# A two-block transformer kernel: operands of 16 and 64 rows become zero-padded operands of 128 rows

## The chip, the cores and the metric

The kernel runs on one core of a Trainium2 chip. The metric is device time in microseconds (us) of one execution, lower is better. Engines are named as in the profile: PE is the matrix engine (PEld its weight loads), DVE, ACT and POOL work on vectors, SP issues the DMAs.

## The reference

Two blocks run one after the other over 512 tokens with 16 meta tokens ahead of them (L = 528), width 1024, all in float32.

```python
def first_block(...):                       # two layers
    for i in range(2):
        xn = rms_norm(h, attn_norm[i])
        gq, gk, gv, gr, glr, fq, fk, fv, ff = split(xn @ w_in[i])
        log_a = log_sigmoid(glr @ w_alpha_up[i] + b_alpha[i]) / 16   # contracts over 16
        o_gla = gla_chunk_causal(gq, gk, gv, log_a)                  # 4 heads, chunks of 64 tokens
        log_f = log_sigmoid(ff + b_forget[i])
        o_fox = forgetting_attention(fq, fk, fv, log_f)              # 8 heads of 64, causal softmax
        h = h + concat(norm(o_gla) * silu(gr), norm(o_fox)) @ w_out[i]
        h = h + conv_ffn(rms_norm(h, ffn_norm[i]), ...)

def second_block(...):                      # one layer
    q, k, v, qi, ki, wi, cu, cb, cc, ga, gb = split(rmsnorm(h) @ w_in)
    score = einsum(relu(qi . ki), wi)       # 8 index heads of 64 features
    sel = top_k(score, 128)                 # keys that each query may see
    y_attn = softmax(q . k over sel) . v    # 8 heads of 128
    h = h + mixed(y_attn, short_conv branch) @ w_out
    h = h + gated_ffn(h)
```

## The kernel before

**Large products.** Each projection is a job: one 128-column tile of a weight matrix against all tokens, in `steps` (L291 to L322). Float32 operands are cut into a high and a low part of type fp32r, and each job adds hi*hi, hi*lo and lo*hi in one PSUM tile `mm`, at L309. A job of two 264-column halves and eight 128-row steps issues 48 matmuls.

**Side work.** Everything else (attention, gates, norms) is a queue of small functions. After every step of a job `pump` takes functions from that queue (a credit of `rate` for each step), so small products stand between the large ones on the same in-order PE. The tile framework's scheduler may shift an instruction a little; `pin` holds one in place. Operands lie in a pool of 64 slots of [128, 528] (`G`), small PSUM tiles in two pools of two (`PS`, `PT`).

**Small products with fewer than 128 rows.** A matmul contracts over the rows (partitions) of its two operands.

- Forgetting attention (FoX), four pairs of heads in each of two layers. A head has 64 features. `stacked_scores` (L494) does two matmuls: L497 has 128 rows (high and low queries stacked, keys' high parts in both halves), L498 has 64 rows (queries' high parts against the keys' low parts, which share one tile `kl` for both heads). L558 then adds the causal mask as a bf16 product of 128 rows. There is one unit of that kind for each head and query block: 2 heads x 5 blocks x 4 pairs x 2 layers = 80 units.
- FoX values (L608): two products over the 16 meta keys (`vms`, 16 rows) come first, then two of 128 rows for each key block, all in one PSUM tile. 32 such groups.
- FoX meta queries: a 16x16 transpose (L568) and a 16-row product (L574, a float32 product, which the engine runs as two instructions), 16 units.
- Index scores (L1070) use `stacked_scores` too, 40 times; nothing but large products follows.
- Attention of block 2: `attend_p` (L451) transposes each key block of the probabilities (L459) and the meta keys apart (L467, 16 columns); the product with the meta values (`dvm`, 16 rows) comes last at L1120, as two instructions, 32 groups.
- Gates (L391, 16 rows), the first block of each norm spread (L210, 16 rows) and the meta block in `fox_tail` (L669, 16 rows).

GLA's own products (L695, L709, L753, L760) have 16 or 64 rows too, and so have the transposes at L1561, L783 and L1191.

POOL zeroes the meta block of the FoX output tile (L524) and one block of the values' operand (L582) and does a few additions and powers. It works in order.

Of the kernel before, what the change touches and what calls it, by code (L numbers as in the profile page):

```python
# [8 lines left out]
F32 = mybir.dt.float32  # L9
# [6 lines left out]
META = 16  # L16
# [20 lines left out]
class Net:  # L37
# [43 lines left out]
    # ---------------------------------------------------------------- constants  # L81
    def constants(self):
# [26 lines left out]
        self.wa = c.tile([16, 2, 256], F32, name="wa")  # L109
# [48 lines left out]
    # ---------------------------------------------------------------- small helpers  # L158
# [34 lines left out]
    def token_sums(self, acc):  # L193
        """Per-token sums over the features: [128, 5], one column a token block."""
# [6 lines left out]
    def spread(self, r):  # L201
        """[128, L] tile with r's per-token values in every partition."""
# [3 lines left out]
        for j, (b, sz) in enumerate(BLK):  # L206
            dg = self.M()
            nc.vector.tensor_scalar(dg[:sz, :sz], self.ident[:sz, :sz], r[:sz, j:j + 1], None, op0=ALU.mult)
            t, o = (tiles[0], b) if b < HALF else (tiles[1], b - HALF)
            nc.tensor.matmul(t[:, o:o + sz], lhsT=self.ones[:sz, :], rhs=dg[:sz, :sz], start=True, stop=True)  # L210
# [10 lines left out]
    def norm_at(self, first, sums, spread):  # L221
        """A phase's norm factors, made while its first two jobs run: sums late in the first, spread in the second."""
# [4 lines left out]
    # ---------------------------------------------------------------- weight jobs  # L227
# [17 lines left out]
    def split(self, jb, pin=False):  # L245
        """High and low parts of a job's weights; a packed job has both in one tile, 64 columns each."""
# [20 lines left out]
    def push_unit(self, stages):  # L267
        """Stages of one unit of side work; each stage goes one unit later than the stage before it."""
# [22 lines left out]
    def steps(self, jb):  # L291
        """One job's matrix products, a step for each 128 rows of the weights, then its evacuation."""
# [31 lines left out]
    def run(self, look=2, ahead=4):  # L324
        """The jobs in order; the first two go together, as their operand comes in bit by bit."""
# [25 lines left out]
    def v(t, toks):  # L351
        """View of a [128, L] tile that matches psv of the same tokens."""
# [8 lines left out]
    def scaled(self, ps, toks, rs, out=None, extra=None):  # L361
        """ps * rs (* extra) over the tokens, into a slot."""
# [76 lines left out]
    def to_tokens(self, src, dst, dmeta, mcol, eng):  # L439
        """[128 features, L] -> four 128-token blocks side by side, and the meta rows."""  # L440
# [10 lines left out]
    def attend_p(self, P, j, qs, vt, vm, mcol, vw, vc):  # L451
        """Transposes of the probabilities' key blocks; gives (lhsT-ready) blocks."""
        nc = self.nc
        blocks = []
        if j:
            pt = self.PT("attend_pT_")
            for k in range(1, j + 1):
                b, _ = BLK[k]
                nc.tensor.transpose(pt[:, 128 * (k - 1):128 * (k - 1) + qs], P[:qs, b:b + 128],  # L459
                                    self.ident[:qs, :qs])  # L460
            PTs = self.G()
            self.copy("a" if j % 2 else "v", PTs[:, :128 * j], pt[:, :128 * j])
            for k in range(1, j + 1):
                blocks.append((PTs[:, 128 * (k - 1):128 * (k - 1) + qs],
                               vt[:, 128 * (k - 1) + vc:128 * (k - 1) + vc + vw]))
        pm = self.PT("attend_pT_")
        nc.tensor.transpose(pm[:META, :qs], P[:qs, :META], self.ident[:qs, :qs])  # L467
        PM = self.M()
        self.copy("v", PM[:META, :qs], pm[:META, :qs])
        blocks.append((PM[:META, :qs], vm[:META, mcol:mcol + vw]))  # L470
        return blocks

    def fox_k(self, st, t):
        """Per head: the keys' high parts in both row halves; the low parts of both heads in one tile."""
        nc = self.nc
        st["kl"] = kl = self.G(F32R)
        st["kh"] = []
        for b in range(2):
            R, O = slice(64 * b, 64 * b + 64), slice(64 - 64 * b, 128 - 64 * b)
            kh = self.G(F32R)  # L480
# [3 lines left out]
            st["kh"].append(kh)  # L484

    def stack_q(self, t, b, t0=0):
        """One head's queries: high parts in its own rows, low parts in the other rows."""
# [6 lines left out]
    def stacked_scores(self, ps, q, kh, kl, b, q0, a, n, stop):  # L494
        """Query rows q0.. against keys a..a+n, as high and low parts."""
        R = slice(64 * b, 64 * b + 64)
        self.nc.tensor.matmul(ps[:, :n], lhsT=q[:, q0:q0 + 128], rhs=kh[:, a:a + n], start=True, stop=False)  # L497
        self.nc.tensor.matmul(ps[:, :n], lhsT=q[R, q0:q0 + 128], rhs=kl[R, a:a + n], start=False, stop=stop)  # L498
# [1135 lines left out]
```

## Time and profile before

| | |
|---|---|
| timed runs, median of 3 | 2444.22 us (2442.56 to 2447.89) |
| profiled execution, span from first to last instruction | 2443.0 us |
| PE busy | 2411.0 us, 99% of the span |
| DVE, ACT, POOL busy | 1372.8, 942.0, 228.7 us |
| granted PE clock, mean | 0.994 of full speed |

The profile gives the span of its execution and no other time for it; the span lies 1.2 us under the median of the timed runs. A busy PE is not a PE at its peak: matmuls overlap, and the duration of one (some 280 ns for 264 columns) is not what it adds to the time. What it adds is read from the starts: from the start of one matmul to the start of the next.

### The profile page before, as it was taken

The page shows a single profiled execution, that of the slowest core. Times are in us where ns is not written, and L with a number is a line of the kernel's source. Part 1 is how long each engine was busy: PE and PEld are TensorE (multiplying, and loading weights), DVE is VectorE, ACT ScalarE, POOL GpSimd, SP SyncE. Part 2 cuts the span into 40 slices and gives each one's busy share as a digit, 9 for nine tenths or more (in the row PEclk, how much of TensorE's full clock was granted, in tenths as well). Part 3 has the DMA queues.
Part 4 walks back from the last instruction along what each step waited for, and adds up shares of the span by engine and source line. Part 5 has one row for each costly group of instructions (what it writes and reads, how often), then busy time and mean ns, then how long its engine had stood idle before and what let it go on. Part 6 is the DMA issues. An engine that isn't in the chain of part 4 may idle for free.

```text
span 2443.0 us, 37854 instructions
## 1 busy us (share of the span) xinstructions
PE 2411.0 (99%) x15831; PEld 2154.9 (88%) x15831; DVE 1372.8 (56%) x2492; ACT 942.0 (39%) x1609; POOL 228.7 (9%) x216
## 2 busy tenths in 40 slices
PE   7999999999999999999999999999999999999998
PEld 6888999999998888999898988888898888888888
DVE  6556656555555666566464664688344544433335
ACT  6553434333345544434232443332233523222225
POOL 1010110000021101200000031110000002101012
PEclk9999999999998999999999999999999999999999
DMA  4211122232331111222323222232221132232233
GB/s 123 57 53 36 53 87 87 91 100 78 100 85 52 49 39 53 70 87 87 104 83 100 81 90 70 70 104 87 87 69 53 56 100 87 88 102 87 95 99 126
DMA packets 217074, 196.79 MB, mean 81 GB/s; under 512 B 8987, under 2 KB 214791, under 8 KB 216903
## 3 DMA queue, kind: packets, MB, share of 16 engines
q1 hardware_dynamic: 216903, 194.37, 25.7%
q8 instruction: 125, 2.05, 0.4%
q14 instruction: 46, 0.38, 0.1%
HBM read 192.26 MB, written 2.10 MB: 80 GB/s over the span
## 4 chain that ended last, share of the span: by engine, by line
PE 67%; ACT 1%; issue 1%; DVE 1%; POOL 0%; DMA 0%; POOLq 0%; ACTq 0%; SPq 0%; DVEq 0%
PE mm L309 59%; PE valuesT L1120 1%; PE foxV L608 1%; PE scoresS L1103 1%; PE foxS L498 1%; PE idx L498 1%; PE gla_statesS L709 0%; PE foxT L588 0%; PE attend_pT L459 0%; PE spreadS L210 0%; ACT wh L260 0%; PE foxS L497 0%; PE idx L497 0%; PE to_tokensT L445 0%; PE foxS L558 0%
## 5 line engine op out<-in xcount | busy, mean ns | idle before, releaser
L309 PE MATMUL mm<-g,wh 128*128 128x264 f32 (+3 forms) x9168 | 1890.1, 316 | 6.8 <-DVE g L365 4.5
L309 PEld LDWEIGHTS mm<-g,wh 128*128 128x128 f32 x9168 | 1389.5, 190 | 124.2 <-issue 9.8
L309 PE MATMUL mm<-g,wl 128*128 128x264 f32 (+3 forms) x4552 | 1161.8, 313 | 0.0
L309 PEld LDWEIGHTS mm<-g,wl 128*128 128x128 f32 x4552 | 751.3, 189 | 51.6 <-issue 0.3
L260 ACT ACTIVATE wh<-raw 128x1024 fp32r<-128x1024 f32 (+1 forms) x369 | 384.6, 1043 | 978.6 <-PE mm L309 831.2
L261 DVE TENSOR_TENSOR wl<-raw,wh 128x1024 fp32r<-128x1024 f32 (+1 forms) x369 | 444.8, 1206 | 83.1 <-ACT wh L260 58.1
L365 DVE TENSOR_TENSOR g<-mm,g 128x528 f32<-128x528 f32 (+2 forms) x228 | 158.6, 696 | 327.5 <-PE mm L309 324.2
L191 POOL TENSOR_TENSOR g<-g,g 128x528 f32<-128x528 f32 (+3 forms) x49 | 71.5, 1470 | 911.8 <-ACT g L190 911.8
L166 DVE TENSOR_TENSOR g<-g,g 128x512 fp32r<-128x512 f32 (+3 forms) x131 | 91.5, 698 | 39.9 <-ACT g L972 29.0
L997 DVE TENSOR_TENSOR g<-mm,g 128x528 f32<-128x528 f32 (+1 forms) x48 | 33.6, 700 | 118.7 <-PE mm L309 118.6
L954 ACT ACTIVATE g<-g,cv 128x528 f32<-128x528 f32 (+1 forms) x88 | 72.1, 820 | 17.6 <-DVE g L365 17.6
L166 DVE TENSOR_TENSOR g<-foxT,g 16x128 fp32r<-16x128 f32 (+2 forms) x160 | 49.8, 335 | 42.9 <-ACT g L593 35.9
L957 DVE SCALAR_TENSOR_TENSOR g<-g,cv,g 128x526 f32<-128x526 f32 (+1 forms) x88 | 66.8, 760 | 3.1
L956 DVE SCALAR_TENSOR_TENSOR g<-g,cv,g 128x527 f32<-128x527 f32 (+1 forms) x88 | 66.3, 753 | 1.8 <-ACT g L954 1.8
L1383 POOL TENSOR_TENSOR g<-g,g 128x512 f32<-128x512 f32 x22 | 38.9, 1767 | 283.1 <-ACT g L1382 283.1
L968 ACT ACTIVATE g<-g 128x528 f32<-128x528 f32 (+1 forms) x44 | 28.1, 639 | 84.0 <-DVE g L957 84.0
L174 POOL TENSOR_TENSOR sm<-sm,mhalf 128x10 f32<-128x10 f32 (+4 forms) x29 | 36.8, 1279 | 192.5 <-DVE sm L173 192.1
L563 ACT ACTIVATE g<-g,sm 128x144 f32<-128x144 f32 (+2 forms) x80 | 41.4, 517 | 21.1 <-DVE sm L559 18.3
L593 ACT ACTIVATE g<-foxT 128x256 fp32r<-128x256 f32 (+1 forms) x96 | 32.8, 342 | 42.8 <-PE foxT L588 36.8
L970 DVE TENSOR_TENSOR g<-g,g 128x528 f32<-128x528 f32 (+1 forms) x44 | 30.8, 701 | 32.3 <-ACT g L968 32.3
L972 ACT ACTIVATE g<-g 128x528 fp32r<-128x528 f32 (+1 forms) x44 | 28.1, 639 | 33.1 <-DVE g L970 33.1
L1414 DVE TENSOR_TENSOR g<-mm,g 128x512 f32<-128x512 f32 x16 | 11.1, 692 | 50.2 <-PE mm L309 50.2
(264 smaller groups left out, 1699.0 us busy)
## 6 DMA issues: line engine op xcount, KB each, us to landing
raw<-in_w_up_dram SPq DMA_DIRECT2D x50, 1024.0 KB
raw<-in_w_in_dram SPq DMA_DIRECT2D x44, 1024.0 KB
raw<-in_w_down_dram SPq DMA_DIRECT2D x28, 896.0 KB
raw<-in_w_in_dram SPq DMA_DIRECT2D x28, 512.0 KB
raw<-in_w_out_dram SPq DMA_DIRECT2D x12, 1024.0 KB
raw<-in_w_down_dram SPq DMA_DIRECT2D x12, 1024.0 KB
raw<-in_w_gate_dram SPq DMA_DIRECT2D x10, 1024.0 KB
raw<-in_w_up_dram SPq DMA_DIRECT2D x10, 512.0 KB
```

Of the source, the lines that this page charges most:

```text
L166: (eng or self.nc.vector).tensor_tensor(out, x, hi.bitcast(F32), op=ALU.subtract)
L191: nc.gpsimd.tensor_tensor(acc[:, t0:t1], tmp[:, t0:t1], acc[:, t0:t1], op=ALU.add)
L260: keep(nc.scalar.activation(hi[:, :K], src, AF.Copy))
L261: keep(nc.vector.tensor_tensor(lo[:, :K], src, hi[:, :K].bitcast(F32), op=ALU.subtract))
L309: nc.tensor.matmul(ps[:, b, :n], lhsT=w[:, k, :], rhs=x[:, t:t + n], start=(ki == 0 and pi == 0), stop=(ki == len(order) - 1 and pi == len ...
L365: self.nc.vector.tensor_tensor(self.v(out, toks), self.psv(ps, toks), self.v(rs, toks), op=ALU.mult)
L498: self.nc.tensor.matmul(ps[:, :n], lhsT=q[R, q0:q0 + 128], rhs=kl[R, a:a + n], start=False, stop=stop)
L563: nc.scalar.activation(P[:qs, :N], P[:qs, :N], AF.Exp, scale=-1.0, bias=m, accum_out=col)
L954: nc.scalar.activation(A[:, lo:], U[:, lo:], AF.Identity, bias=self.vec("cb", 44 * i + t), scale=cw(2))
L956: nc.vector.scalar_tensor_tensor(A[:, s1:], U[:, s1 - 1:L - 1], cw(1), A[:, s1:], op0=ALU.mult, op1=ALU.add)
L957: nc.vector.scalar_tensor_tensor(A[:, s0:], U[:, s0 - 2:L - 2], cw(0), A[:, s0:], op0=ALU.mult, op1=ALU.add)
L1383: nc.gpsimd.tensor_tensor(z[:, META:], z[:, META:], self.rs[:, META:], op=ALU.mult)
```

## The change

Every operand named above gets 128 rows; the rows that were not there are zero, or meet a zero row of the other operand.

- `fox_k` makes one `kl` tile for each head, and POOL zeroes its other half (16 more memsets of 64x528, one more slot for each pair). L498 then has 128 rows.
- The meta values `fvm`, `fvms`, `dvm` are constant tiles of 128 rows, zeroed once by POOL at the start, of which rows 0 to 15 are written later. The probabilities that meet them are transposed 128 columns wide in place of 16.
- The meta-query unit works on 128 queries (its mask, softmax and transpose are 128 wide); the 16 that count are kept.
- `attend_p` transposes blocks of 128 columns only, up to four in one PSUM tile, the meta block first.
- Gates: `wa` has 128 rows, zero from row 16, and POOL zeroes rows 64 to 127 of `sm`. Spread and `fox_tail`: 128 rows.

GLA's own products and the transposes of the first tokens stay as they are.

```diff
+        self.wa = c.tile([128, 2, 256], F32, name="wa")
+        nc.gpsimd.memset(self.wa, 0.0)
+        for x in range(2):
+            self.fvm.append(c.tile([128, 128], F32, name=f"fvm{x}"))
...
+                nc.gpsimd.memset(t.bitcast(F32), 0.0)
...
-            nc.tensor.matmul(t[:, o:o + sz], lhsT=self.ones[:sz, :], rhs=dg[:sz, :sz], start=True, stop=True)
+            nc.tensor.matmul(t[:, o:o + sz], lhsT=self.ones, rhs=dg[:, :sz], start=True, stop=True)
...
-                nc.tensor.matmul(ps[:, :n], lhsT=self.wa[:, i, 128 * m:128 * m + 128], rhs=sm[:16, a:a + n],
+                nc.tensor.matmul(ps[:, :n], lhsT=self.wa[:, i, 128 * m:128 * m + 128], rhs=sm[:, a:a + n],
...
+        for x in range(0, j + 1, 4):
+            n = min(4, j + 1 - x)
             pt = self.PT("attend_pT_")
...
+            for k in range(n):
+                nc.tensor.transpose(pt[:, 128 * k:128 * k + 128], P[:, cols[x + k]:cols[x + k] + 128], self.ident)
...
         for b in range(2):
-            kh = self.G(F32R)
+            kh, kl = self.G(F32R), self.G(F32R)
+            nc.gpsimd.memset(kl[O, :].bitcast(F32), 0.0)
...
-        self.nc.tensor.matmul(ps[:, :n], lhsT=q[R, q0:q0 + 128], rhs=kl[R, a:a + n], start=False, stop=stop)
+        self.nc.tensor.matmul(ps[:, :n], lhsT=q[:, q0:q0 + 128], rhs=kl[:, a:a + n], start=False, stop=stop)
...
-        q0, qs = BLK[j]
+        q0, qs = BLK[j] if j else (0, 128)
...
-            nc.tensor.transpose(pm[:META, :META], u["P"][:META, :META], self.ident[:META, :META])
+            nc.tensor.transpose(pm[:, :128], u["P"][:, :128], self.ident)
...
-            nc.tensor.transpose(pm[:META, :128], u["P"][:, :META], self.ident)
+            nc.tensor.transpose(pm[:, :128], u["P"][:, :128], self.ident)
...
-                b, sz = BLK[j]
-                self.pin(nc.tensor.transpose(pt[:, b - t0:b - t0 + sz], O[:sz, j, :], self.ident[:sz, :sz]))
+                b = BLK[j][0] - t0
+                self.pin(nc.tensor.transpose(pt[:, b:b + 128], O[:, j, :], self.ident))
...
+            nc.gpsimd.memset(sm[64:, :], 0.0)
```

The order of the large products hardly moves. Two places matter.

POOL, before, between the second and the third pair of FoX heads in the first layer: L582 zeroes operand blocks, L524 the output tile of a later pair, L174 is a norm's power.

```order
L174 TENSOR_TENSOR sm_1409<-sm_1411,mhalf 128x10
L582 TENSOR_TENSOR g_1441<-ident 128x128
L582 TENSOR_TENSOR g_1443<-ident 128x128
L582 TENSOR_TENSOR g_1504<-ident 128x128
L582 TENSOR_TENSOR g_1506<-ident 128x128
L582 TENSOR_TENSOR g_1604<-ident 128x128
L582 TENSOR_TENSOR g_1607<-ident 128x128
L582 TENSOR_TENSOR g_1690<-ident 128x128
L582 TENSOR_TENSOR g_1693<-ident 128x128
L524 MEMSET o_2659 128x128
L174 TENSOR_TENSOR sm_2056<-sm_2058,mhalf 128x10
```

The same place on POOL now (L585, L527 and L183 are the three lines above; L484 zeroes the other half of a `kl`).

```order
L183 TENSOR_TENSOR sm_1427<-sm_1429,mhalf 128x10
L585 TENSOR_TENSOR g_1459<-ident 128x128
L585 TENSOR_TENSOR g_1461<-ident 128x128
L585 TENSOR_TENSOR g_1522<-ident 128x128
L585 TENSOR_TENSOR g_1524<-ident 128x128
L585 TENSOR_TENSOR g_1622<-ident 128x128
L585 TENSOR_TENSOR g_1625<-ident 128x128
L585 TENSOR_TENSOR g_1708<-ident 128x128
L585 TENSOR_TENSOR g_1711<-ident 128x128
L484 MEMSET g_1775 64x528
L484 MEMSET g_1781 64x528
L527 MEMSET o_2677 128x128
```

The two new memsets stand ahead of the output tile's memset, not behind it.

PE, before, one FoX unit of the first pair: the two score products, the mask, the transposes of another unit, large products.

```order
L497 MATMUL foxS_907<-g_651,g_714 128x272
L498 MATMUL foxS_907<-g_650,g_714 128x272
L558 LDWEIGHTS identb
L558 MATMUL foxS_907<-maskb,identb 128x128
L588 MATMUL foxT_918<-ident,g_876 128x128
L596 MATMUL foxT_922<-ident,g_876 16x128
L309 MATMUL mm_781<-g_338,wh_659 128x264 x2
```

The same unit now (L501, L502, L561, L591, L599 and L318 are the lines above).

```order
L501 MATMUL foxS_925<-g_668,g_735 128x272
L502 MATMUL foxS_925<-g_669,g_735 128x272
L561 LDWEIGHTS identb
L561 MATMUL foxS_925<-maskb,identb 128x128
L591 MATMUL foxT_936<-ident,g_894 128x128
L599 MATMUL foxT_940<-ident,g_894 128x128
L318 MATMUL mm_802<-g_355,wh_680 128x264 x2
```

Nothing moved there; the second score product reads its head's own `kl`, and the last transpose is 128 wide.

## Rows read from the trace of the kernel before

**Rows 1.** The page, busy time of each engine, its share of the span.
```profile
PE 2411.0 (99%) x15831; PEld 2154.9 (88%) x15831; DVE 1372.8 (56%) x2492; ACT 942.0 (39%) x1609; POOL 228.7 (9%) x216
```

**Rows 2.** Waits: who waited for whom, us in total, times, longest.
```profile
DVE g L365 <- PE mm L309: 324.2, 132, 3.8
...
POOL o L524 <- DVE sm L649: 177.4, 5, 44.9
```

**Rows 3.** Timeline of PE, FoX, first pair: start, us, what, how many merged.
```profile
89.76 0.49 PE L588 MATMUL foxT<-ident,g 128*128 128x128 f32 x3
90.09 0.27 PE L596 MATMUL foxT<-ident,g 128*16 128x128 f32 x1
90.11 0.61 PE L309 MATMUL mm<-g,wh 128*128 128x264 f32 x3
90.57 0.41 PE L309 MATMUL mm<-g,wl 128*128 128x264 f32 x2
90.81 0.34 PE L497 MATMUL foxS<-g,g 128*128 128x400 f32 x1
```

**Rows 4.** Timeline of PE, FoX, second pair: two score units.
```profile
134.57 0.39 PE L498 MATMUL foxS<-g,g 64*128 64x272 f32 x1
134.89 0.39 PE L309 MATMUL mm<-g,wh 128*128 128x264 f32 x1
135.12 0.28 PE L497 MATMUL foxS<-g,g 128*128 128x256 f32 x1
135.33 0.38 PE L498 MATMUL foxS<-g,g 64*128 64x256 f32 x1
135.64 0.23 PE L558 MATMUL foxS<-maskb,identb 128*128 128x128 bf16 x1
```

**Rows 5.** Timeline of PEld, index scores: the load of one 64-row product.
```profile
1500.35 0.18 PEld L498 LDWEIGHTS idx<-g,g 64*128 64x128 f32 x1 [0.26 <-issue]
```

**Rows 6.** PE at L498: count; duration min, median, max in ns; first, last start.
```profile
L498 PE MATMUL foxS<-g,g x96: 379/387/592, 72.2 to 962.4; 64*128 64x256 f32 x48, 64*128 64x272 f32 x32, 64*128 64x400 f32 x16
...
L498 PE MATMUL idx<-g,g x40: 379/387/450, 1463.4 to 1552.2; 64*128 64x256 f32 x16, 64*128 64x272 f32 x16, 64*128 64x400 f32 x8
```

**Rows 7.** Timeline of PE: one FoX values group.
```profile
189.86 0.49 PE L608 MATMUL foxV<-g,vms 16*128 16x256 f32 x2
190.29 1.22 PE L608 MATMUL foxV<-g,g 128*128 128x256 f32 x8
191.34 0.40 PE L309 MATMUL mm<-g,wl 128*128 128x264 f32 x2
```

**Rows 8.** Timeline of PE: the end of one values group of block 2.
```profile
1845.01 0.50 PE L1120 MATMUL valuesT<-g,g 128*128 128x128 f32 x3
1845.44 0.48 PE L1120 MATMUL valuesT<-md,dvm 16*128 16x128 f32 x2
1845.85 0.76 PE L309 MATMUL mm<-g,wh 128*128 128x264 f32 x4
1846.45 0.41 PE L309 MATMUL mm<-g,wl 128*128 128x264 f32 x2
```

**Rows 9.** Timeline of PE: the 16x16 transpose of a meta-query unit.
```profile
73.86 0.18 PE L568 MATMUL foxT<-ident,g 16*16 16x16 f32 x1
73.97 0.39 PE L309 MATMUL mm<-g,wh 128*128 128x264 f32 x1
74.19 0.41 PE L309 MATMUL mm<-g,wl 128*128 128x264 f32 x2
```

**Rows 10.** Busy time by stretch: length, PE, PEld, DVE, ACT, POOL, clock, DMA.
```profile
72.00:79.00 7.00, 7.00 (x44) 5.11 (x45) 2.37 (x16) 1.92 (x10) 0.00 (x0) 1.00 0.48 132
...
782.00:790.00 8.00, 8.00 (x34) 6.07 (x33) 2.02 (x10) 2.10 (x7) 0.00 (x0) 0.57 0.05 11
```

**Rows 11.** Timeline of POOL: L582 of the second pair of the first layer.
```profile
120.38 3.70 POOL L582 TENSOR_TENSOR g<-ident 128x128 fp32r<-128x128 f32 x8
```

**Rows 12.** Timeline of PE: the first 64-row score product of the third pair.
```profile
157.43 0.38 PE L498 MATMUL foxS<-g,g 64*128 64x256 f32 x1
```

More of the change, by code (lines that the diff above doesn't have):

```diff
@@ L108, in constants @@
         self.bf = c.tile([40, 2], F32, name="bf")
-        self.wa = c.tile([16, 2, 256], F32, name="wa")
+        self.wa = c.tile([128, 2, 256], F32, name="wa")
+        nc.gpsimd.memset(self.wa, 0.0)
+        self.fvm, self.fvms, self.dvm = [], [], []
+        for x in range(2):
+            self.fvm.append(c.tile([128, 128], F32, name=f"fvm{x}"))
+            self.fvms.append([c.tile([128, 128], F32R, name=f"fvms{x}{b}") for b in range(2)])
+            self.dvm.append(c.tile([128, 128], F32, name=f"dvm{x}"))
+            for t in (self.fvm[x], self.fvms[x][0], self.fvms[x][1], self.dvm[x]):
+                nc.gpsimd.memset(t.bitcast(F32), 0.0)
     def vectors(self):
@@ L449, in to_tokens, with attend_p @@
         self.copy("v", dmeta[:META, mcol:mcol + 128], pm[:META, :128])
-    def attend_p(self, P, j, qs, vt, vm, mcol, vw, vc):
+    def attend_p(self, P, j, vt, vm):
         nc = self.nc
+        cols = [0] + [BLK[k][0] for k in range(1, j + 1)]
+        vals = [vm] + [vt[:, 128 * k:128 * k + 128] for k in range(j)]
         blocks = []
-        if j:
+        for x in range(0, j + 1, 4):
+            n = min(4, j + 1 - x)
             pt = self.PT("attend_pT_")
[L457 to L470, printed above, removed]
+            for k in range(n):
+                nc.tensor.transpose(pt[:, 128 * k:128 * k + 128], P[:, cols[x + k]:cols[x + k] + 128], self.ident)
+            PTs = self.G() if n > 1 else self.M()
+            self.copy("v" if x or j % 2 else "a", PTs[:, :128 * n], pt[:, :128 * n])
+            blocks += [(PTs[:, 128 * k:128 * k + 128], vals[x + k]) for k in range(n)]
         return blocks
@@ L484, in fox_k @@
             st["kh"].append(kh)
+            st["kl"].append(kl)
     def stack_q(self, t, b, t0=0):
@@ L515, in fox_prep @@
         nc.tensor.transpose(pm[:META, :128], st["fv"][:, :META], self.ident)
-        st["vm"] = self.meta.tile([META, 128], F32, tag="vm", bufs=2, name=self.n("vm"))
-        nc.vector.tensor_copy(st["vm"], pm[:META, :128])
-        st["vms"] = [self.meta.tile([META, 128], F32R, tag=f"vms{b}", bufs=2, name=self.n("vms")) for b in range(2)]
+        st["vm"], st["vms"] = self.fvm[p % 2], self.fvms[p % 2]
+        nc.vector.tensor_copy(st["vm"][:META], pm[:META, :128])
         for b in range(2):
             C = slice(64 * b, 64 * b + 64)
-            nc.scalar.activation(st["vms"][b][:, :64], pm[:META, C], AF.Copy)
-            self.lo_sub(st["vms"][b][:, 64:], pm[:META, C], st["vms"][b][:, :64])
+            nc.scalar.activation(st["vms"][b][:META, :64], pm[:META, C], AF.Copy)
+            self.lo_sub(st["vms"][b][:META, 64:], pm[:META, C], st["vms"][b][:META, :64])
         st["O"] = self.opool.tile([128, 5, 128], F32, tag="o", name=self.n("o"))
@@ L555, in scores @@
                 last = a + n == N
-                self.stacked_scores(ps, st["q"][b], st["kh"][b], st["kl"], b, q0, a, max(n, 256), not last)
+                self.stacked_scores(ps, st["q"][b], st["kh"][b], st["kl"][b], q0, a, max(n, 256), not last)
                 if last:
@@ L573, in trans_meta @@
             o = self.PT("foxV_")
-            nc.tensor.matmul(o[:META, :64], lhsT=PM[:META, :META], rhs=st["vm"][:, r:r + 64], start=True, stop=True)
+            nc.tensor.matmul(o[:, :64], lhsT=PM, rhs=st["vm"][:, r:r + 64], start=True, stop=True)
             nc.vector.tensor_scalar(st["O"][:META, 0, r:r + 64], o[:META, :64], rc[:META, 0:1], None, op0=ALU.mult)
@@ L595, in trans @@
             pm = self.PT("foxT_")
[L596 to L598 removed]
+            nc.tensor.transpose(pm[:, :128], u["P"][:, :128], self.ident)
+            nc.scalar.activation(group["m"][:, 0, C], pm[:, :128], AF.Copy)
+            self.lo_sub(group["m"][:, 1, C], pm[:, :128], group["m"][:, 0, C])
         def values():
@@ L1113, in trans @@
         def trans():
-            u["blocks"] = self.attend_p(u["P"], j + 1, 128, d["vt"], d["vm"], 0, 128, 0)
+            u["blocks"] = self.attend_p(u["P"], j + 1, d["vt"], d["vm"])
         def values():
@@ L1290, in prep @@
                     d["vt"] = self.G()
-                    d["vm"] = self.meta.tile([META, 128], F32, tag="dvm", bufs=2, name=self.n("dvm"))
+                    d["vm"] = self.dvm[h % 2]
                     self.to_tokens(d["v"], d["vt"], d["vm"], 0, "a")
```

18 lines of the change are left out of this document (7 added, 11 removed).

## The prediction

> **What bounds the kernel now.** I read the page first: PE is busy for 2411.0 of 2443.0 us, DVE for 56% [rows 1]. The waits say the same from the other side: the evictions of the large products wait for PE 132 times and 324.2 us in all, at most 3.8 us at once [rows 2]. So what PE saves comes off the end, and what another engine gains or loses is covered while it stays behind PE. But 99% is not PE at its peak. A product of 264 columns is shown with some 0.28 us; two of them take 0.24 us from the first start to the next matmul's start (90.57 to 90.81) [rows 3], so one costs 0.12 us. The timeline is therefore read by starts, and what I look for is a start that comes later than this pace.
>
> It comes later around every product with 64 or 16 rows. In [rows 4], L497 (128 rows, 256 columns) starts at 135.12 and the 64-row L498 at 135.33: 0.21 us where 0.12 is the pace. From L498 to the mask it is 0.31 us, in the case above to a large product 0.32 us, and that large product itself takes 0.23 us until the next start (134.89 to 135.12). The load of such a product's weights begins only with the product itself; PEld sat idle for 0.26 us ahead of one, and no other engine is named as the cause [rows 5]. Between products of 128 rows the loads run ahead and this idle time is absent. So a change of the row count costs on three intervals: before the small product, after it, and one later.
>
> **The change part by part.** All terms compare starts with the pace of 0.12 us for 256 to 272 columns.
>
> *Second score product (L498).* It runs 96 times in FoX and 40 times in the index scores [rows 6]. Where the mask follows (80 units), the excess is 0.21 - 0.12 = 0.09 before and 0.31 - 0.12 = 0.19 after: 0.28 us. The mask's own interval I leave as it is. In the other 56 a product of full pace follows, and its 0.23 - 0.12 = 0.11 joins: 0.09 + 0.19 + 0.11 = 0.39 us. The sum is 80 x 0.28 + 56 x 0.39 = 22.4 + 21.8 = 44.2 us. All of it lies on PE, the engine that sets the end.
>
> *FoX meta values (L608).* The two 16-row products take 0.43 us (189.86 to 190.29) where two at pace take 0.24; the eight after them take 1.05 us (to 191.34) where eight take 0.96 [rows 7]. With 0.09 before the first, as at L498, that is 0.19 + 0.09 + 0.09 = 0.37 us, 32 times: 11.8 us.
>
> *Meta values of block 2 (L1120).* These are float32 products of 128 columns. The nearest full pace is that of the 128-column transposes, three in 0.33 us, 0.11 each [rows 3]. Three full products ahead of the small pair take 0.43 us, 0.10 too much; the pair takes 0.41 us where 0.22 is the pace; the four large products after it take 0.60 us where they need 0.48 [rows 8]. The last 0.12 may belong to any float32 product that goes over to fp32r: it goes or it stays. I take a quarter, since after the change a float32 product still stands last. So 0.10 + 0.19 + 0.03 = 0.32 us, bounds 0.29 and 0.41, 32 times: 10.2 us, bounds 9.3 and 13.1.
>
> *The meta-query unit, gates, spreads, tail.* Around the 16x16 transpose the intervals are 0.11 and then 0.22 us [rows 9]; with 0.09 before it, it costs 0.09 + 0.11 + 0.10 = 0.30 where a full transpose costs 0.11. That is 0.19 us for each of 16, 3.0 us. The 16-row product of the same unit (two instructions) I price the same, 3.0 us. For the groups of L391, L210 and L669, some 20 in all, the nearest rows are these and L608's 0.37; at 0.25 us they give 5.0 us, bounds 3.8 and 7.4. Together 11.0 us.
>
> *What is added.* 96 transposes (64 in FoX, 32 in `attend_p`) go from 16 columns to 128. The row says that this is free: three of 128 columns take 0.33 us, then the narrow one starts; from it to the large product pass 0.02 us, and the three large products after it take 0.46 us where 0.37 is the pace (90.09 to 90.57) [rows 3]. So the narrow one costs 0.02 + 0.09 = 0.11 us, as much as a wide one. The Trainium skill, "TensorE: Matmul & The Clock Gate", section LDWEIGHTS, speaks against this: a load's time goes with its columns, whatever the rows. By its figure of columns over 1.2 in ns, my estimate is 0.09 us more for each of the 96, 9 us, and the sum would end 9 us later; the row decides here.
>
> POOL zeroes a half of `kl` 16 times. No such memset is in the trace; the nearest row is L582, eight of 128x128 in 3.70 us, 0.46 us each [rows 11], and four times its columns give 1.9 us, so 30 us at most in all on an engine that is idle for 91% of the span [rows 1]. The danger is the queue: L524 waits for DVE up to 44.9 us [rows 2], and what stands behind it waits too. In the changed order the two memsets of the third pair stand ahead of it, right after L582 of the second, which ends at 124.1 us [rows 11]; that pair's first small score starts at 157.43 [rows 12]. 33 us of cover: cost nothing. The nine memsets at the start lie before any other work of POOL. The 128-wide softmax of the 16 meta units gives DVE and ACT a few tenths of a us each, behind PE. `attend_p` makes fewer copies than before, on engines that are not late: nothing.
>
> *Two things with bounds only.* The mask behind a 128-row L498 might cost less than the 0.12 us that I left it; 0 to 0.06 us for 80 is 0 to 5 us. And PE's clock: in 782 to 790 us, among FoX's first scores of layer 2, the granted clock is 0.57 of full speed, so most of that stretch ran at 1.2 GHz in place of 2.4, with 34 matmuls in 8 us where the same work of layer 1 had 44 in 7 us at 1.00 [rows 10]. At that rate 34 take 5.4 us, so 2.6 us are lost, and they come back if full-row products keep the clock up. For both I take 2 us of the 0 to 7.6.
>
> **Sum.** 44.2 + 11.8 + 10.2 + 11.0 + 2 = 79.2 us, or 80. Against the profiled span of 2443.0 us that is 2363; the median of the runs lies 1.2 us higher, so **2364 us**, 3.3% faster. Its own range is 2352 to 2378.
>
> **The rivals.** *Followers become late (2391).* PE has hardly any wait in FoX now because each softmax chain has a whole unit's time. A unit becomes 0.3 to 0.7 us shorter while DVE and ACT do as much as before. If the chain then comes last, FoX keeps half of its gain. FoX's share is about 96 x 0.31 + 11.8 + 6 + 3 = 51 us, half of it 26: 2364 + 27 = 2391. Against it: DVE is busy for 56% [rows 1].
>
> *More comes back (2350).* The bounds above at their far ends, 5.6 us more, and further stretches at the low clock like that of [rows 10], of which two more would give some 5 us and the upper bounds of L1120 and the gates the rest: 2364 - 14 = 2350.
>
> *Nothing changes (2444).* The late starts might belong to the places (PSUM tiles, operand types) and not to the rows; padding then buys nothing. Against it stands [rows 7]: same line, same PSUM tile, same type and columns, and only the 16-row pair is slow. The Trainium skill has a rule on this side: "TensorE: Matmul & The Clock Gate", section "Why this matters for your kernels", says that a lone product of 32 rows takes as long as one of 128, and that few rows pay only when several run at once on different row groups. By that rule padding is worth 0.
>
> *Slower (2505).* One more slot of 64 is held for each FoX pair. If the evictions of FoX's 24 query, key and value jobs had to wait for a slot, PE would stand still with both `mm` tiles full. At one job of 48 products, 48 x 0.12 = 5.8 us, for each of the 24, 24 x 5.8 = 139 to 141 us are lost, and 2364 + 141 = 2505. It decides from 80 / 24 = 3.3 us a job. Against it: the evictions wait for PE, 3.8 us at the longest [rows 2].
>
> **How the numbers follow.** Forecast 0.63; followers late 0.16; more comes back 0.13; nothing 0.04; slower 0.04. The first three hold 0.92. The range of 8 in 10 reaches from 2342 (past 2350, by the size of the bounds) to 2392 (past 2391) and leaves out the last two cases and part of the tails. A measurement of this kernel can tell about 0.2% (5 us) from no change. Faster by more 0.93, within 0.03, slower 0.04.
>
> **What would show it.** In the profile of the changed kernel, L497, L498's successor and the mask should follow each other by some 0.12 us, the pair of meta values by 0.12 each, and PEld should have no idle time ahead of them. FoX, index scores and the values of block 2 should each be shorter by their terms (some 51, 15 and 10 us), the plain FFN stages unchanged. I am wrong on the term of a line if its starts stay apart by 0.2 us or more; wrong on the path if the starts close up but PE then waits for DVE or ACT in FoX; wrong on POOL if PE waits for L484.

## The result and the profile after

The changed kernel takes 2372.8 us (median of four runs, 2370.32 to 2373.64), the kernel before beside it 2443.39 (2440.77 to 2447.89). The ratio is 0.971, with an interval of 0.969 to 0.972: 2.9% faster, 70.6 us. The forecast was 2364 us and 3.3%; the range of 2342 to 2392 holds the time.

PE is still the engine that sets the end. The page's first part, busy time of each engine and its share of the span, answers to [rows 1].

```profile
PE 2338.4 (99%) x15831; PEld 2141.2 (90%) x15831; DVE 1373.3 (58%) x2468; ACT 945.8 (40%) x1609; POOL 238.6 (10%) x243
```

PE is busy 72.6 us less with the same number of matmuls, and DVE and ACT do what they did. The waits (who waited for whom, us in total, times, longest) answer to [rows 2].

```profile
DVE g L374 <- PE mm L318: 320.7, 132, 3.8
...
POOL o L527 <- DVE sm L652: 142.8, 5, 34.8
```

The evictions still wait for PE, 3.8 us at the longest: no chain behind the large products has become late.

PE's timeline in the first pair of FoX heads (start, us, what, how many merged) answers to [rows 4] and [rows 9]. L501, L502 and L561 are the two score products and the mask, L571 and L577 the transpose and the product of the meta-query unit.

```profile
73.28 0.28 PE L501 MATMUL foxS<-g,g 128*128 128x256 f32 x1
73.40 0.28 PE L502 MATMUL foxS<-g,g 128*128 128x256 f32 x1
73.52 0.23 PE L561 MATMUL foxS<-maskb,identb 128*128 128x128 bf16 x1
73.56 0.74 PE L318 MATMUL mm<-g,wh 128*128 128x264 f32 x4
74.14 0.28 PE L318 MATMUL mm<-g,wl 128*128 128x264 f32 x1
74.26 0.27 PE L571 MATMUL foxT<-ident,g 128*128 128x128 f32 x1
74.29 0.37 PE L318 MATMUL mm<-g,wl 128*128 128x264 f32 x1
74.50 0.28 PE L501 MATMUL foxS<-g,g 128*128 128x256 f32 x1
...
74.98 0.37 PE L577 MATMUL foxV<-fvm,md 128*128 128x64 f32 x2
75.16 0.61 PE L318 MATMUL mm<-g,wh 128*128 128x264 f32 x3
```

From the first score product to the second pass 0.12 us, to the mask 0.12 more; these were 0.21 and 0.31 in [rows 4]. The starts have closed up to the pace of the large products. PEld, whose 0.26 us of idle time ahead of the small load stood in [rows 5], shows none ahead of L502 in the index scores:

```profile
1464.91 0.19 PEld L501 LDWEIGHTS idx<-g,g 128*128 128x128 f32 x1
1465.03 0.19 PEld L502 LDWEIGHTS idx<-g,g 128*128 128x128 f32 x1
1465.21 0.61 PEld L318 LDWEIGHTS mm<-g,wh 128*128 128x128 f32 x4
```

A FoX values group answers to [rows 7], the start of a values group of block 2 to [rows 8] (the product with the meta values is first in its group now). Both are from PE's timeline.

```profile
130.27 0.28 PE L318 MATMUL mm<-g,wl 128*128 128x264 f32 x1
130.43 0.47 PE L611 MATMUL foxV<-g,fvms 128*128 128x256 f32 x2
130.74 1.11 PE L611 MATMUL foxV<-g,g 128*128 128x256 f32 x8
131.69 0.49 PE L454 MATMUL to_tokensT<-ident,g 128*128 128x128 f32 x3
...
1700.21 0.38 PE L1124 MATMUL valuesT<-g,dvm 128*128 128x128 f32 x2
1700.43 0.39 PE L1124 MATMUL valuesT<-g,g 128*128 128x128 f32 x2
1700.57 0.71 PE L318 MATMUL mm<-g,wh 128*128 128x512 f32 x2
```

In block 2 the meta pair takes 0.22 us, the pace, where it took 0.41. In FoX the two meta products take 0.31 us (130.43 to 130.74), better than 0.43, but not the 0.24 of two at pace.

To see where the time went I compared when the same large product starts in both traces. Layer 1's attention is 19.9 us shorter and the start of its FFN 1.3 us longer; layer 2's attention is 23.9 us shorter, the index scores 15.5, block 2's attention 13.4. With some tenths of a us in the other stages these make up the 71.1 us between the spans (2443.0 and 2371.9). Layer 2 gained 4.0 us more than layer 1, most of it by the clock: a stretch at 1.2 GHz went in layer 2 (worth some 2.6 us), and a longer one near 50 us costs layer 1 some 1.1 us. The windows (length, busy time of PE, PEld, DVE, ACT, POOL, granted clock, DMA share, GB/s) answer to [rows 10].

```profile
50.00:57.20 7.20, 5.53 (x26) 5.45 (x27) 5.55 (x12) 4.00 (x7) 6.04 (x6) 0.53 0.00 0
319.90:323.30 3.40, 3.40 (x17) 3.40 (x17) 0.73 (x4) 0.00 (x0) 1.18 (x1) 0.50 0.02 5
...
782.00:790.00 8.00, 8.00 (x69) 7.83 (x68) 5.84 (x17) 4.67 (x13) 0.00 (x0) 1.00 0.47 128
```

The stretch at 1.2 GHz of layer 2 (782 to 790 us, 0.57 before) is gone; the same work runs some 20 us earlier now, and no stretch lies there either (the nearest ends at 740 us). But the one near 50 us has doubled, from 3.4 to 6.8 us, and there is a new one of 3.4 us at 320, in an FFN that had none: it is the 1.3 us that layer 1 gives back. Apart from the very end, PE ran at 1.2 GHz for 23.9 us before and 23.9 us after.

### The profile page after: what moved, and what is told of

It is laid out like the page before. It is cut to its first block, busy times and chain, and to the rows that moved or that the text cites. A ratio compares the mean times of both kernels' runs of the same rounds, so it can differ in the third digit from the quotient of the medians.

```text
span 2371.9 us, 37876 instructions
## 1 busy us (share of the span) xinstructions
PE 2338.4 (99%) x15831; PEld 2141.2 (90%) x15831; DVE 1373.3 (58%) x2468; ACT 945.8 (40%) x1609; POOL 238.6 (10%) x243
## 4 chain that ended last, share of the span: by engine, by line
PE 67%; ACT 1%; issue 1%; DVE 1%; POOL 0%; DMA 0%; POOLq 0%; ACTq 0%; SPq 0%
PE mm L318 60%; PE valuesT L1124 1%; PE scoresS L1107 1%; PE foxV L611 1%; PE attend_pT L471 1%; PE gla_statesS L712 0%; PE foxT L591 0%; ACT wh L269 0%; POOL g L200 0%; PE foxS L501 0%; PE spreadS L219 0%; PE to_tokensT L454 0%; PE foxS L502 0%; DMA raw<-in_w_down_dram 0%; PE idx L501 0%
## 5 line engine op out<-in xcount | busy, mean ns | idle before, releaser
L318 PE MATMUL mm<-g,wh 128*128 128x264 f32 (+3 forms) x9168 | 1881.9, 316 | 7.1 <-DVE g L374 4.8
L318 PEld LDWEIGHTS mm<-g,wh 128*128 128x128 f32 x9168 | 1391.1, 190 | 110.9 <-issue 7.0
L318 PE MATMUL mm<-g,wl 128*128 128x264 f32 (+3 forms) x4552 | 1162.3, 313 | 0.0
L318 PEld LDWEIGHTS mm<-g,wl 128*128 128x128 f32 x4552 | 751.7, 189 | 50.5
L175 DVE TENSOR_TENSOR g<-g,g 128x512 fp32r<-128x512 f32 (+3 forms) x131 | 92.3, 704 | 39.1 <-ACT g L976 29.1
L175 DVE TENSOR_TENSOR g<-foxT,g 128x128 fp32r<-128x128 f32 (+1 forms) x160 | 49.6, 338 | 21.1 <-ACT g L596 19.6
L183 POOL TENSOR_TENSOR sm<-sm,mhalf 128x10 f32<-128x10 f32 (+4 forms) x29 | 36.8, 1280 | 161.3 <-DVE sm L182 161.0
L562 DVE CUSTOM_DVE_ANT_0 g<-foxS,g 128x144 f32<-128x144 f32 (+2 forms) x80 | 32.3, 404 | 14.7 <-PE foxS L561 14.0
```

What stands on the lines that cost most here:

```text
L175: (eng or self.nc.vector).tensor_tensor(out, x, hi.bitcast(F32), op=ALU.subtract)
L183: self.nc.gpsimd.tensor_tensor(out, v[:rows, :n], self.mhalf[:rows, :n], op=ALU.pow)
L318: nc.tensor.matmul(ps[:, b, :n], lhsT=w[:, k, :], rhs=x[:, t:t + n], start=(ki == 0 and pi == 0), stop=(ki == len(order) - 1 and pi == len ...
```

## Experiments

Each kernel was timed beside the kernel before, whose median lay between 2441.7 and 2444.4 us. Intervals are for the ratio to the kernel before. None of these kernels leaves out a part of the computation; the two with extra transposes do some work twice, and the one with 96 rows adds a small term, named there.

### Each part taken back alone

**Score products.** In the changed kernel, the second score product contracts over 64 rows again.

```diff
+        R = slice(64 * b, 64 * b + 64)
...
-        self.nc.tensor.matmul(ps[:, :n], lhsT=q[:, q0:q0 + 128], rhs=kl[:, a:a + n], start=False, stop=stop)
+        self.nc.tensor.matmul(ps[:, :n], lhsT=q[R, q0:q0 + 128], rhs=kl[R, a:a + n], start=False, stop=stop)
```

> The changed kernel, but the second score product of FoX and of the index scores has its 64 rows again (136 products); the separate kl tiles and their memsets stay. Theory (a product over 64 rows or fewer delays the starts around it): the trace shows 0.09 us before, 0.19 after, 0.11 for the next product again; some 42 us come back (26 in FoX, 15.5 in the index stage, which took 74 us for its 500 large products before and 71 now), 2415 us. Rival (the gain came from the separate kl tiles, a changed order or the places, not from the rows): 2373 us.

Measured: 2413.54 us, ratio 0.988 (0.986 to 0.989), 40.7 us over the changed kernel. By the starts of the same large products, FoX is 24.2 us longer and the index scores 15.3. The late starts are back in the timeline of PE (L502, L503 and L562 are the score products and the mask here):

```profile
154.51 0.38 PE L502 MATMUL foxS<-g,g 128*128 128x256 f32 x1
154.82 0.38 PE L503 MATMUL foxS<-g,g 64*128 64x256 f32 x1
155.13 0.23 PE L562 MATMUL foxS<-maskb,identb 128*128 128x128 bf16 x1
155.17 0.37 PE L318 MATMUL mm<-g,wl 128*128 128x264 f32 x1
```

The `kl` tiles, places and neighbours are those of the changed kernel; only the rows differ. So the late starts belong to the rows, and the score products carry more than half of the gain.

**FoX meta values.**

```diff
-            ops = [(vms, group["m"][:, 0, :]), (vms, group["m"][:, 1, :])]
+            ops = [(vms[:META], group["m"][:META, 0, :]), (vms[:META], group["m"][:META, 1, :])]
```

> The changed kernel, but the two products of FoX values over the meta keys contract over 16 rows again (32 groups); everything else as changed. Theory: 0.25 to 0.37 us for each group, 8 to 12 us, 2381 to 2385 us. Rival (in the changed kernel the second of the pair waits for DVE's low part anyway, so a slow pair hides behind that wait): under 5 us, 2375 to 2377 us.

Measured: 2382.72 us, ratio 0.975 (0.974 to 0.976), 9.9 us over the changed kernel: inside what the theory expected, outside the rival's.

**Meta values of block 2.** The meta product stands first in its group, as in the changed kernel, but over 16 rows.

```diff
+                r = slice(0, META) if x == 0 else slice(0, 128)
-                nc.tensor.matmul(o[:, :128], lhsT=rv, rhs=lt, start=x == 0, stop=x == len(bl) - 1)
+                nc.tensor.matmul(o[:, :128], lhsT=rv[r], rhs=lt[r], start=x == 0, stop=x == len(bl) - 1)
```

> The changed kernel, but the product with the meta values in block 2's attention contracts over 16 rows again (32 pairs; it now stands first of its group, not last). Theory: 0.40 us for each, 13 us, 2386 us, with nothing lost from its place. Rival (part of the 13 us came from attend_p's fewer copies and the changed place in the group): 2379 to 2382 us.

Measured: 2384.70 us, ratio 0.976 (0.974 to 0.977), 11.9 us over the changed kernel. PE's timeline of one group:

```profile
1893.74 0.39 PE L318 MATMUL mm<-g,wl 128*128 128x512 f32 x1
1894.06 0.48 PE L1125 MATMUL valuesT<-g,dvm 16*128 16x128 f32 x2
1894.47 0.71 PE L1125 MATMUL valuesT<-g,g 128*128 128x128 f32 x4
```

The small pair takes 0.41 us again, as in [rows 8], although it now stands first: nearly all of the price goes with the rows, and about 1 us at most with the place in the group.

**All three at once.** The edits are the three above.

> The changed kernel with three of its parts taken back at once: score products, FoX meta products and block-2 meta products contract over few rows again, as before. If the parts' worths add up, the three single undos (40.7, 9.9 and 11.9 us) make 62.5 us, and this kernel takes 2372.8 + 62.5 = about 2435 us; the parts that stay (meta queries, gates, norm spreads) are then worth the remaining 8. If the worths overlap, because a late start of one product hides another's, it stays clearly under 2430 us. If they strengthen each other, it comes near the kernel before, 2443, and the parts that stay are worth nothing.

Measured: 2434.43 us, ratio 0.996 (0.995 to 0.998), 61.6 us over the changed kernel, where the three single ones add up to 62.5. The worths add. The 8.8 us that still lie between this kernel and the one before (2443.24 beside it) belong to the meta queries, the gates, the spreads, the tail and the new place of block 2's meta product. They are known to some 3 us only: the profile of this kernel has 17.0 us at 1.2 GHz in place of 23.9, so a part can be the clock's.

### How many rows are few

In the kernel **before**, the second product of every other index head contracts over rows 0 to 95 (rows 64 to 95 hold low parts of the queries, so for 32 features a product of low parts is added that the kernel before leaves out).

```diff
-        R = slice(64 * b, 64 * b + 64)
+        R = slice(0, 96) if wide else slice(64 * b, 64 * b + 64)
```

> The kernel before, but the second index-score product of the four even heads contracts over 96 rows (20 of the 40 products; the extra 32 rows add a low-times-low part). Theory that the engine treats over 64 rows as full: those 20 run at the pace, 20 x 0.39 us, 7.8 us less than before, 2435.6 us, and the other 20 stay late. Rival (any operand short of 128 rows is late, in proportion or in full): 2440 to 2443 us. In the trace the start after a 96-row product comes at 0.12 us by the first and at 0.2 to 0.3 us by the second.

Measured: 2437.72 us, ratio 0.997 (0.996 to 0.998); the index stage is 7.8 us shorter than before, as the theory had it, and half of what full padding gave there. The loads at that line of the source (durations min, median, max in ns; 20 with 96 rows, 20 with 64), and one product of 96 rows in PE's timeline:

```profile
L498 PEld LDWEIGHTS idx<-g,g x40: 182/185/192, 1463.0 to 1543.7; 96*128 96x128 f32 x20, 64*128 64x128 f32 x20
...
1467.18 0.28 PE L497 MATMUL idx<-g,g 128*128 128x256 f32 x1
1467.30 0.28 PE L498 MATMUL idx<-g,g 96*128 96x256 f32 x1
1467.42 0.65 PE L309 MATMUL mm<-g,wh 128*128 128x258 f32 x4
```

96 rows are as good as 128: 0.12 us on both sides. The 64-row products of the other heads still keep 0.31 to 0.32 us to the next start. What costs is not a row that is missing but a product of 64 rows or fewer among larger ones. The loads show the same step: in this run the load of each 64-row product starts 1 or 2 ns ahead of its product, and the load behind it at most 5 ns ahead of its own, while the loads of the 96-row products and of those behind them run some 0.12 us ahead. The Trainium skill, "TensorEngine Tiling (Array Packing)", section Key Properties, has a rule that fits: changing the tiling mode drains TensorE. The page has modes of 128, 64 and 32 rows, and 96 rows fit the first alone. These runs show the steps at 64 and 96 rows and their price; that it is a drain they do not show.

### Two 64-row products side by side

The kernel **before**, with its index heads taken in pairs: both 128-row products, then the two 64-row ones, on rows 0 to 63 and rows 64 to 127, in two PSUM tiles. Nothing is padded.

```diff
+                for b in range(2):
+                    self.pin(nc.tensor.matmul(ps[b][:, :m], lhsT=qi[h + b][:, q0:q0 + 128], rhs=box["kh"][:, a:a + m], start=True, stop=False))
+                for b in range(2):
+                    H = slice(64 * b, 64 * b + 64)
+                    self.pin(nc.tensor.matmul(ps[b][:, :m], lhsT=qi[h + b][H, q0:q0 + 128], rhs=box["kl"][H, a:a + m], start=False, stop=True))
```

> The kernel before, with its index heads' score products taken two heads at a time: both 128-row products, then both 64-row products next to each other, one on rows 0 to 63, one on rows 64 to 127, in different banks. Nothing is padded. If the second 64-row product starts 0.22 us behind the first, as the second 16-row product of the rows read before did, a pair saves about 0.28 us of its late starts, 5.6 us in all for 20 pairs: 2438 us. If a second one on other rows is not late at all (0.12 us behind the first), the pair saves 0.4 us: about 2435 us. If the two run at the same time, the second starts nearly together with the first, and the pair saves about 0.5 us: about 2433 us. The distance of the starts of the two 64-row products in the trace tells it.

Measured: 2437.05 us, ratio 0.998 (0.997 to 0.999), 6.2 us under the kernel before. In the trace the index stage alone is 9.5 us shorter; about 1 us is given back later in the program, where nothing was changed, and the two profiled spans differ by 7.7 us; the rest is within the spread of the runs. PE and PEld in one pair:

```profile
1473.35 0.40 PE L1071 MATMUL idx<-g,g 128*128 128x256 f32 x2
1473.67 0.39 PE L1074 MATMUL idx<-g,g 64*128 64x256 f32 x2
1473.99 0.75 PE L309 MATMUL mm<-g,wh 128*128 128x258 f32 x4
...
1473.67 0.19 PEld L1074 LDWEIGHTS idx<-g,g 64*128 64x128 f32 x2
```

The two 64-row products together take 0.39 us, as long as one alone. Their records start 3 to 5 ns apart in 19 of the 20 pairs (a large product came between the two of the other), and their loads 3 to 4 ns. They run at the same time, as the third expectation had it; its saving of 0.5 us for each pair is there in the index stage (9.5 us for 20), its 2433 us are not reached. This agrees with the Trainium skill, "TensorE: Matmul & The Clock Gate", section "Why this matters for your kernels", which has products on different row groups start within 4 ns of each other. It still saves less here than padding (9.5 against 15.5 us in the same stage): the 0.32 us behind the pair is still there, and the four large products after it take 0.59 us to the next start (1474.58 in the trace) where they need 0.48.

### Why the second meta product of FoX is still late

In the changed kernel the first `fvms` product of a group is mostly followed after 0.19 us (median), not 0.12. Either the meta probabilities come late, or it is an after-effect of whatever stands ahead of the group. Here the meta products go last in the group.

```diff
-            ops = [(vms, group["m"][:, 0, :]), (vms, group["m"][:, 1, :])]
+            ops = []
...
+            ops += [(vms, group["m"][:, 0, :]), (vms, group["m"][:, 1, :])]
```

> The changed kernel, but in FoX values the two meta products come after the key blocks' products. Theory (in the changed kernel PE waits there for ACT's and DVE's parts of the meta probabilities, which are made last and used first: the start between the two is 0.19 us at the median where 0.12 is the pace): 32 x 0.07 us and something before the first, 2 to 4 us, 2369 to 2371 us. Rival (that spacing is no wait but a cost of the place): 2373 us, and the 0.19 us stays.

Measured: 2373.74 us, ratio 0.971 (0.970 to 0.973): no gain. PE's timeline of the same group as above:

```profile
130.14 1.19 PE L612 MATMUL foxV<-g,g 128*128 128x256 f32 x8
131.17 0.40 PE L612 MATMUL foxV<-g,fvms 128*128 128x256 f32 x2
131.41 0.60 PE L454 MATMUL to_tokensT<-ident,g 128*128 128x128 f32 x4
```

The meta pair now takes 0.24 us, the pace, and the eight ahead of it take 1.03 us in place of 0.95. The lateness went to whichever product is second in the group: over all 32 groups 1.6 us moved from the meta products to the others.

There is a wait in it all the same, one of the loads. In 16 of the 32 groups, in the changed kernel and here alike, the first load of the group starts some 0.05 us after a subtraction on DVE ends (L175, which makes the low parts of the probabilities). DVE and PEld at one such group, in the changed kernel and then here:

```profile
88.65 0.62 DVE L175 TENSOR_TENSOR g<-foxT,g 128x256 fp32r<-128x256 f32 x2 [0.35 <-ACT g L596]
89.33 0.30 PEld L611 LDWEIGHTS foxV<-g,fvms 128*128 128x128 f32 x2
```
```profile
88.28 0.62 DVE L175 TENSOR_TENSOR g<-foxT,g 128x256 fp32r<-128x256 f32 x2 [0.37 <-ACT g L596]
88.96 0.42 PEld L612 LDWEIGHTS foxV<-g,g 128*128 128x128 f32 x3
```

In the changed kernel these 16 groups have their second start at 0.19 us on average. In eight others the first load runs 0.12 us ahead of its product, and the second start comes at 0.12. Of the last eight, at 0.19 to 0.20 us, six stand right behind the float32 product of the meta queries and two behind another wait. So a load that starts late is paid one interval later. The theory named the right engine, but the edit doesn't take the wait away: the first load still waits for DVE when the meta products stand last. Why it does, although its own product reads nothing of the meta part, isn't settled.

### Narrow or wide transposes

The changed kernel does one more transpose in each of 64 FoX units, its result unused, 128 columns wide or 16.

```diff
+            nc.tensor.transpose(pm[:, 128:256], u["P"][:, :128], self.ident)
```
```diff
+            nc.tensor.transpose(pm[:META, 128:256], u["P"][:, :META], self.ident)
```

> The changed kernel with one more transpose for each of 64 FoX units: the first 128 columns of the probabilities once more, into unused columns of the same PSUM tile. By the rows (a wide transpose costs 0.11 us): 64 x 0.11 = 7 us more, 2380 us.

> The same with a narrow one: 16 columns, as the kernel before had them. By the rows (a narrow one costs 0.11 us too): 7 us more, 2380 us, the same as the wide one. By the Trainium skill's rule that a weight load's time goes with its columns: 0.09 us less for each of the 64, 6 us less than the wide one, 2374 us.

Measured: wide 2388.67 us, ratio 0.977 (0.976 to 0.979); narrow 2385.89, ratio 0.977 (0.975 to 0.978). PE's timeline of the narrow one (L599 is the extra transpose):

```profile
112.03 0.27 PE L591 MATMUL foxT<-ident,g 128*128 128x128 f32 x1
112.14 0.27 PE L599 MATMUL foxT<-ident,g 128*16 128x128 f32 x1
112.25 0.27 PE L600 MATMUL foxT<-ident,g 128*128 128x128 f32 x1
```

Both kinds take 0.11 us from start to start. Up to the same large product near the end, the wide one costs 11.4 us and the narrow one 11.3; the 2.8 us between their times arise behind it. So the zero for going from 16 to 128 columns holds. The Trainium skill, "TensorE: Matmul & The Clock Gate", section LDWEIGHTS, has a load's time go with its columns; here that time (0.09 us for 16 columns and 0.14 for 128 in PEld's records) lies beside the running matmul and is not in the spacing. Both times lie over the 2380 us that were expected, by 8.7 and 5.9 us. The total is more than 64 x 0.11 = 7.0 us: some 2 us more lie in FoX's score units, the rest elsewhere and in the last stage, where the order shifted a little and the wide kernel has a stretch at 1.2 GHz. I can't split that further.

### The same cure where the change left it out

GLA's state products still contract over 64 and 16 rows. Here they get two zero-padded tiles of 128 rows for each pair of heads, as `kl` did.

```diff
-        kt = self.G()
+        kt = [self.G(), self.G()]
+        nc.gpsimd.memset(kt[0][64:, :512], 0.0)
+        nc.gpsimd.memset(kt[1][:64, :512], 0.0)
...
-                    nc.tensor.matmul(ps[:, 128 * b:128 * b + 128], lhsT=st["kt"][m][R0:R0 + 64, C],
-                                     rhs=st["gvt"][2 * m + b][R0:R0 + 64, C], start=True, stop=True)
+                    nc.tensor.matmul(ps[:, 128 * b:128 * b + 128], lhsT=st["kt"][m][c % 2][:, C],
+                                     rhs=st["gvt"][2 * m + b][:, C], start=True, stop=True)
```

> The changed kernel, and GLA's state products, which still contract over 64 or 16 rows (L712, 128 instructions in 32 groups, and L698 in 4), get 128 rows: two zero-padded tiles in place of one for the keys, km and gvm constant. Theory: each group now costs 0.09 before it, 0.08 after, 0.10 once more and something within: 0.3 us, 36 times, 11 us, 2362 us. Rival (the extra copies and memsets on ACT and POOL, or the slots, cost more than that): 2373 us or more.

Measured: 2362.47 us, ratio 0.967 (0.965 to 0.968), 10.3 us under the changed kernel. PE's timeline of two state products (four instructions), in the changed kernel and then here:

```profile
180.35 0.71 PE L712 MATMUL gla_statesS<-g,g 64*128 64x128 f32 x4
180.98 0.76 PE L318 MATMUL mm<-g,wh 128*128 128x264 f32 x4
181.58 0.40 PE L318 MATMUL mm<-g,wl 128*128 128x264 f32 x2
```
```profile
180.58 0.61 PE L722 MATMUL gla_statesS<-g,g 128*128 128x128 f32 x4
180.94 0.73 PE L322 MATMUL mm<-g,wh 128*128 128x264 f32 x4
```

Four instructions take 0.36 us in place of 0.63; over both layers the state products' own starts give 8.5 us (from 23.0 to 14.5). The profile has 17.0 us at 1.2 GHz in place of 23.9, so a part of the other 1.8 can be the clock's. The same rule, used on another part of the program, forecast 11 us and 10.3 were measured: this version beats both kernels. With the meta products last as well, nothing is added:

> Both edits of the two runs beside it. By the theories of both the gains add: 13 to 15 us less than the changed kernel, 2358 to 2360 us. If either rival holds, the time of the other alone.

Measured: 2363.65 us, ratio 0.967 (0.966 to 0.969), the same as `gla_padded` alone within the spread of the runs.

## Why the prediction was right, and where its sizes were off

**The mechanism held.** A product over 64 or 16 rows between 128-row ones costs on the intervals before and behind it and one later, and padding takes that away. Each single undo brings its stretch back, and the three add.

| Term | Forecast, us | Measured, us | From |
|---|---|---|---|
| score products, FoX | 28.6 | 24.2 | starts, undo of scores |
| score products, index | 15.6 | 15.3 | starts, undo of scores |
| FoX meta values | 11.8 | 9.9 | undo |
| block-2 meta values | 10.2 | 13.0 | starts, after against before (11.9 by the undo, which keeps the new place) |
| meta queries, gates, spreads, tail | 11.0 | some 7 | starts of those products |
| mask and clock | 2 | 0 | trace of after |

(The forecast's 44.2 for the scores is split here: 80 x 0.28 + 16 x 0.39 = 28.6 in FoX, 40 x 0.39 = 15.6 in the index scores.) The measured column adds up to some 69 us of the 70.6; the forecast's was 79.2.

- *FoX scores, 4.4 too high.* FoX's own score and mask starts gave 26.0 us, where 96 x 0.28 = 26.9 were forecast. The failing step is the neighbours: for the sixteen products without a mask behind them, 0.11 us of the next product were to be won too, 1.8 in all, but, by the undo, the neighbours lost 1.7 in sum (0.9 at the meta values, 0.4 at `foxN`, 0.7 at large products, with 0.3 won at the transposes).
- *FoX meta values, 1.9 too high.* After the change the second product of the group is still late, 0.19 us in the median. The forecast took all starts to the pace and put DVE's part at nothing. In the 16 groups whose first load waits for DVE (L175), the starts of the first and the second product stay late by some 2.2 us in sum; the run with the meta products last shows that any product in that place takes it.
- *Block-2 meta values, 2.8 too low.* Of the last 0.12 us I took a quarter, because a float32 product still stands last. All of it went: the upper bound (13.1) was the right value. The product that stands last goes over to the large ones in 0.03 us, as the transposes in [rows 3] do.
- *Meta-query unit.* The transpose gave what was said: three intervals of 0.55 us became 0.36, 0.2 us each and 3 us in all. The 16-row product priced "the same" did not: its four intervals went from 0.66 us to 0.60 on average (leaving out the unit that ran at 1.2 GHz before), some 1 us in place of 3.0. It was already quick (the two starts of the pair and the next in 0.21 us), and in most units the interval ahead of it stays at 0.13 to 0.33 us after the change, for a reason that no run here settles.
- *Gates, spreads, tail.* Priced at 5.0 us, their own starts gave 2.9: the gates 1.6, the tail 0.8, the spreads 0.5.
- *Clock.* The 2.6 us of [rows 10] came back, as hoped, and were lost at 50 us (some 1.1) and at 320 us (1.3). In the run that takes back the score products, too, nothing is granted 1.2 GHz at that place of layer 2, though it has the 64-row products. So few rows do not by themselves bring the clock down there. The 2 us should have been 0, with a range on both sides of nothing.
- *Costs taken as nothing.* They were nothing: PE nowhere waits for the new memsets (L484, 0.53 us each and 8.5 in all, where up to 30 had been allowed), the slots or `attend_p`, and the wide transposes cost no more than narrow ones.
- *Slips in the working.* Half of FoX's share is 26 where 27 was added, and 24 x 5.8 is 139, not 141: neither changes the range.

**The rivals.** *Followers late* falls: the profile names no wait of PE for DVE or ACT in FoX, and the loads that wait for DVE's L175 cost some 2 us, where that rival had 27. *Nothing changes* falls with the first undo. *Slower*, by slots, falls with the evictions' longest wait, 3.8 us before and after. *More comes back* didn't come either: of its bounds only that of block 2 was reached. The time came out 8.8 us over the forecast for three reasons. Every start was to close up to the pace, and some stayed late: FoX's neighbours, the second product of the meta groups, the interval ahead of the meta-query product. Gates, spreads and tail were priced from rows of other lines. And a stretch of low clock that goes was not set against one that comes. Block 2's meta values, priced too low, took a part of it back.

## What to carry to other kernels

Read a matmul's cost from start to start, and look one interval further than the product you doubt: a product over 64 rows or fewer between 128-row products cost 0.27 to 0.39 us more than a full one here, and the rows of zeros added no time on PE. Pad such operands to 128 rows where one tile can be zeroed once; where two products over half of the rows stand side by side, they run at once, but the change to and from them is still paid. Before a price read at one place is multiplied by a count, take the mean over all places, neighbours included.

## What the runs showed of the hardware that was not expected

- 96 rows behave as 128: starts 0.12 us on both sides, where 64 rows have 0.31 behind them.
- Two 64-row products on different halves of the rows start 3 to 5 ns apart and take 0.39 us together, the time of one; two products on the same 16 rows start 0.22 us apart.
- The rule by which a lone product of few rows takes as long as a full one (the Trainium skill, "TensorE: Matmul & The Clock Gate", section "Why this matters for your kernels") isn't borne out here for a 64-row product among 128-row ones: its own start and the two starts behind it are late, together by 0.27 to 0.39 us.
- The load of a 64-row product starts with the product (1 to 2 ns ahead, all 136 in the kernel before), where the load of a 128-row one starts 0.12 us ahead (median of the large products).
- A first load of a group that is held up costs the next start too: 0.19 us where 0.12 is the pace, in 16 of FoX's 32 values groups.
- An extra transpose of 16 columns costs the 0.11 us of one of 128.
- The stretches at 1.2 GHz moved with small shifts of the work (3.4 us at 320 us in the changed kernel, none there before; in the kernel with padded GLA they are at 315 and 994 us, too), and no part of the program that was changed tells where they fall. Their sum, without the very end, was 23.9 us before and after and 17.0 in that kernel.
